# Hybrid pooling, stick-breaking and memory layer in fp32: memory attention's result parked in DRAM, its slots lent to the scores, and the last head pair's projections and pooling work reordered

## The chip, the cores and the metric

The kernel runs on one core of one Trainium2 chip. The metric is the device time of one execution in microseconds (us). The kernel before was timed three times: 543.44, 544.04 and 546.48 us, median 544.04 us. One more execution of it was taken with the hardware profiler.

## The reference

One decoder layer without its feed-forward half. `x` has 1024 tokens of 1024 channels, fp32. `h` is the RMS-normalised `x`, and one product `h @ W_in` gives all inputs of three mixers, whose outputs, each times SiLU of its gate, are concatenated, multiplied by `W_out` and added to `x`:

```
h = rmsnorm(x);  pool_v, pool_gate, sb_q, sb_k, sb_v, sb_gate, mem_q, mem_gate = split(h @ W_in)
A  pooling (256 channels, 4 groups of 64): windows of 2, 4, 8, 16 tokens:
     y = ((window_sum / count) - u) @ pool_w[group] * pool_scale
B  stick-breaking attention (8 heads of 64), strictly causal:
     z = q k^T / 8;  log_a = log_sigmoid(z) + sum over later keys of log_sigmoid(-z);  y = exp(log_a) @ v
C  memory attention (4 heads of 64): softmax over 256 memory tokens, RMS-normed q and k
out = x + concat(A*silu(gate), B*silu(gate), C*silu(gate)) @ W_out
```

## The kernel before, in words

**Numbers.** Every product is fp32 made of split parts: each operand is a high part plus a low part, and TensorE (PE) does high x high, high x low and low x high. A copy on ScalarE (ACT) makes the high part, a subtraction on VectorE (DVE) or GpSimd (POOL) the low one.

**Stages.** First come the norms, the transposes of `x` and the memory tokens' keys and values. Then memory attention (`mem_main`) runs among the first projections; its result stays in the slots `Y0` and `Y1` as `y_mem`. Then stick-breaking attention runs in four head pairs, p = 0 to 3, among the remaining projections. Last comes the output product, one level of Strassen-like recursion: seven products of 512x512 blocks (`oA`, `oS`, L1256 to L1258). Its sums of blocks are additions on DVE (L1232 `tt`; low parts L1226 `bs` and L1197 `hl`; sums of results L1267), and its operands `b_qa0`, `b_KA0`, `b_KB1` and so on are pieces of `W_out` that SP loads into slots that earlier stages have left (L1210).

**A projection unit** is 128 output columns of `h @ W_in`: two halves of 512 tokens with eight steps each, a step being three matmuls of 128x512 (L251, L254). `chain` loads the next unit's weights (SP, L152) in the first step of a unit, and splits them by quarters in later steps (ACT `wh` L277, POOL `wl` L278). Units are called `q`, `k`, `v`, `g` with the head pair (`v2`), `pv0`, `pv1` (the pooling values, two groups each), `pg0`, `pg1` (pooling gates) and `mg0`, `mg1` (memory gates).

**A score tile** (`be`, one head h, one block tb of 128 tokens, all keys up to it) goes this way. PE: `z` L754. ACT: sigmoid into a `be` buffer, L758. DVE: the running product along the keys, L767. For the head h = 1, DVE then transposes blocks of 32 (L769), SP stores the tile to DRAM (`zd`, L777) and reads it back transposed (`al`, L797 to L803), ACT makes the high part (L822) and POOL the low one (L823). For h = 0, PE transposes it (`ta` L593), ACT and DVE split it (L597, L598). PE: times `v` (`av`, L611). ACT and DVE: the result to `g_g`, where it meets the gate (L630, L633, L634). There are 64 score tiles, 16 for each pair. They take turns in four buffers with the tag `be`: a buffer comes free when its last reader (the store to DRAM, or PE's transposes) is done. Below, x counts score tiles from 0 in the order in which they get a buffer; x = 0 is the first of pair 0, x = 48 the first of pair 3.

**What sets the order.** `weave(main, fill, keep, lag)` puts attention's steps among the projection steps by planned costs: the last `keep` steps of the fill are left for the end, and the attention starts against a `lag`. `soon(us, fn)` defers vector work by planned microseconds. Inside the section `hand`, DVE, ACT, POOL and SP run in the order in which the code issues; behind `flush()` and `hand.close()` a scheduler places the vector work, and it may hoist the output product's work between that of the last pair. Each engine runs its list in order, so whatever waits at its head holds up what follows.

**The last pair** is woven with the units pv1, pg1, pv0, pg0, mg0. `pool_parts(r)` gives the pooling work of the unit pv r. `window_add` makes a window sum of twice the width from the last one: a copy of the first columns (L924, DVE) and an addition (L925). `mean` divides and subtracts (L936 to L939). ACT and POOL split the result (L944 `ph`, L947 `pl`), and `out_step` does the group's product (`py`, L964 to L966), whose result DVE multiplies by the gate (L969). The pooling works in slots that hold the output product's operands afterwards: `us` in `KA0`, `ps2` in `qa0`, `ph` in `qb0`. The unit mg writes a gate by `gate_unit` (L413, L416), and L418 multiplies `y_mem` by it.

Of the kernel before, what the change touches and what calls it, by code (L numbers as in the profile page):

```python
# [27 lines left out]
def layer_kernel(  # L28
# [305 lines left out]
    def k_unit(e0, name, tags):  # L334
        get = lazy(lambda: [slot2(t, f"{t}_{name}", dt=F32R)[:].rearrange("p (n s) -> p n s", n=2) for t in tags])

        def evac(th, c, pt):
# [12 lines left out]
            soon(0.9, low)  # L350
            soon(3.0, copy)

        return get, Unit(e0, name, evac)
# [530 lines left out]
    def pool_parts(r, gg):  # L884
# [27 lines left out]

        todo = []

        def window_add(n, c):
# [4 lines left out]
            prev, cur = (u if n == 0 else (s, s2)[(n - 1) % 2]), (s, s2)[n % 2]  # L920
            lo = HD if n == 2 * r + 1 else 0
            c0 = max(c.start, step)
            if c.start == 0:
                nc.vector.tensor_copy(cur[lo:P, 0:step], prev[lo:P, 0:step])  # L924
            (nc.gpsimd if [0, 0][r] else nc.vector).tensor_tensor(  # L925
                cur[lo:P, c0 : c.stop], prev[lo:P, c0 : c.stop], prev[lo:P, c0 - step : c.stop - step], op=ALU.add
            )
# [448 lines left out]
```

## Time and profile before

| | |
|---|---|
| median of three runs | 544.04 us (543.44 to 546.48) |
| the profiled execution, its own time | 546.15 us |
| span of the profiled execution, first to last instruction | 544.2 us |
| mean granted TensorE clock | 0.977 |
| PE busy | 506.1 us, 93% |
| DVE, ACT, POOL busy | 402.7, 296.5, 245.0 us |
| memory attention to the first scores of pair 0 | about 120 to 138 us |
| stick-breaking attention, pairs 0 to 3 | about 138 to 448 us, the heavy part of each at its end |
| output product | about 464 to 541 us |

The profiled execution took 2.11 us more than the median of the three runs, and 1.95 us of its time lie outside the span. Busy times of an engine are read against the span; a TensorE clock under 1.00 means that matmuls in that stretch ran slower than they can.

### The profile page before, as it was taken

The page shows a single profiled execution, that of the slowest core. Times are in us where ns is not written, and L with a number is a line of the kernel's source. Part 1 is how long each engine was busy: PE and PEld are TensorE (multiplying, and loading weights), DVE is VectorE, ACT ScalarE, POOL GpSimd, SP SyncE. Part 2 cuts the span into 40 slices and gives each one's busy share as a digit, 9 for nine tenths or more (in the row PEclk, how much of TensorE's full clock was granted, in tenths as well). Part 3 has the DMA queues.
Part 4 walks back from the last instruction along what each step waited for, and adds up shares of the span by engine and source line. Part 5 has one row for each costly group of instructions (what it writes and reads, how often), then busy time and mean ns, then how long its engine had stood idle before and what let it go on. Part 6 is the DMA issues. An engine that isn't in the chain of part 4 may idle for free.

```text
span 544.2 us, 7905 instructions
## 1 busy us (share of the span) xinstructions
PE 506.1 (93%) x2548; PEld 419.8 (77%) x2548; DVE 402.7 (74%) x627; ACT 296.5 (54%) x670; POOL 245.0 (45%) x239
## 2 busy tenths in 40 slices
PE   7889999999987999899999899996779989999997
PEld 6678888888865888688888688885657768888886
DVE  4777777786477955789855799558997588999663
ACT  6977756767354645564655465544643636563200
POOL 4570344445312363424745165454474753033980
PEclk9999999999998999989999899999899989999999
DMA  8910112435146633654664638643443432802123
GB/s 308 312 56 22 39 40 67 90 78 108 24 92 146 150 73 106 141 127 90 141 142 114 136 69 152 139 117 61 85 98 106 143 127 80 268 1 89 66 99 134
DMA packets 149504, 60.36 MB, mean 111 GB/s; under 512 B 104006, under 2 KB 139096, under 8 KB 149464
## 3 DMA queue, kind: packets, MB, share of 16 engines
q1 hardware_dynamic: 149464, 59.87, 43.0%
q8 instruction: 20, 0.33, 0.3%
q14 instruction: 20, 0.16, 0.1%
HBM read 39.92 MB, written 15.73 MB: 102 GB/s over the span
## 4 chain that ended last, share of the span: by engine, by line
PE 69%; DVE 9%; ACT 5%; issue 5%; DMA 4%; POOL 4%; SPq 2%; ACTq 0%; POOLq 0%; DVEq 0%
PE av L611 6%; PE u_q L254 5%; PE u_v L254 5%; PE u_g L254 5%; PE z L754 4%; DVE be L767 3%; PE u_k L254 3%; PE u_q L251 3%; PE u_g L251 3%; PE oS L1256 3%; PE oS L1258 3%; PE u_v L251 3%; PE oS L1257 3%; DMA zd<-be 2%; PE u_mg L254 2%
## 5 line engine op out<-in xcount | busy, mean ns | idle before, releaser
L767 DVE TENSOR_TENSOR_SCAN be<-be,later 128x128 f32<-128x128 f32 (+3 forms) x64 | 97.2, 1521 | 27.8 <-ACT be L758 27.2
L823 POOL TENSOR_TENSOR al<-al,ah 128x512 fp32r<-128x512 f32 (+1 forms) x40 | 56.9, 1425 | 71.2 <-ACT ah L822 56.9
L758 ACT ACTIVATE be<-z 128x128 f32<-128x128 f32 (+3 forms) x96 | 46.5, 490 | 64.7 <-PE z L754 27.2
L611 PE MATMUL av<-al,V_v 128*128 128x256 f32 (+1 forms) x160 | 33.3, 291 | 6.9 <-DVE al L598 5.3
L611 PEld LDWEIGHTS av<-ah,V_v 128*128 128x128 f32 x160 | 30.4, 195 | 11.2 <-issue 4.3
L598 DVE TENSOR_TENSOR al<-ta,ah 128x512 fp32r<-128x512 f32 (+1 forms) x40 | 25.2, 631 | 17.1 <-ACT ah L597 11.8
L754 PE MATMUL z<-KB_k,qb_q 128*128 128x512 f32 (+3 forms) x96 | 26.6, 362 | 9.1 <-ACT be L758 9.1
L611 PE MATMUL av<-ah,V_v 128*128 128x256 f32 (+1 forms) x160 | 31.0, 276 | 3.5 <-DVE g_g L634 3.5
L754 PE MATMUL z<-KA_k,qa_q 128*128 128x512 f32 (+3 forms) x96 | 27.3, 368 | 5.8 <-ACT be L758 5.8
L611 PEld LDWEIGHTS av<-al,V_v 128*128 128x128 f32 x160 | 25.1, 195 | 8.8 <-DVE al L598 6.6
L597 ACT ACTIVATE ah<-ta 128x512 fp32r<-128x512 f32 (+1 forms) x40 | 22.2, 556 | 15.8 <-PE ta L593 12.2
L630 ACT ACTIVATE avt<-av,ve_v 64x128 f32<-64x128 f32 x64 | 19.7, 356 | 19.7 <-PE av L611 11.2
L703 POOL TENSOR_SCALAR pe_m<-pe_m,nb_m 128x256 f32<-128x256 f32 x16 | 16.8, 1050 | 27.9 <-DVE nb_m L700 24.1
L754 PEld LDWEIGHTS z<-KB_k,qb_q 128*128 128x128 f32 x96 | 17.4, 193 | 15.4 <-ACT be L758 12.3
L251 PE MATMUL u_g<-hh,wh_g 128*128 128x512 f32 x64 | 27.6, 431 | 0.0
L822 ACT ACTIVATE ah<-al 128x512 fp32r<-128x512 f32 (+1 forms) x40 | 23.4, 584 | 6.6 <-DMA al<-zd 2.0
L251 PE MATMUL u_v<-hh,wh_v 128*128 128x512 f32 x64 | 26.8, 418 | 0.0
L251 PE MATMUL u_k<-hh,wh_k 128*128 128x512 f32 x64 | 26.4, 412 | 0.0
L754 PEld LDWEIGHTS z<-KA_k,qa_q 128*128 128x128 f32 x96 | 18.4, 200 | 10.2 <-ACT be L758 6.3
L278 POOL TENSOR_TENSOR wl_g<-wr_g,wh_g 128x256 fp32r<-128x256 f32 x16 | 13.8, 874 | 27.5 <-ACT wh_g L277 27.3
L1256 PE MATMUL oS<-bs,hh 128*128 128x512 f32 (+1 forms) x68 | 25.9, 381 | 0.0
L1258 PE MATMUL oS<-bs,hl 128*128 128x512 f32 (+1 forms) x68 | 25.8, 379 | 0.0
(322 smaller groups left out, 1601.7 us busy)
## 6 DMA issues: line engine op xcount, KB each, us to landing
al<-zd SPq DMA_DIRECT2D x24, 256.0 KB, 3.2
x<-in_x_dram SPq DMA_DIRECT2D x8, 512.0 KB, 6.3
wr_q<-in_w_in_dram SPq DMA_DIRECT2D x4, 512.0 KB, 4.0
wr_k<-in_w_in_dram SPq DMA_DIRECT2D x4, 512.0 KB, 4.0
wr_v<-in_w_in_dram SPq DMA_DIRECT2D x4, 512.0 KB, 3.8
KA_k<-KA_k SPq DMA_DIRECT2D x8, 256.0 KB, 3.3
KB_k<-KB_k SPq DMA_DIRECT2D x8, 256.0 KB, 3.6
wr_g<-in_w_in_dram SPq DMA_DIRECT2D x4, 512.0 KB, 3.9
```

The source lines that it names most:

```text
L251: nc.tensor.matmul(pt[:], wh[:, kc], hh[k][:, c], start=(k == 0), stop=False)
L254: nc.tensor.matmul(pt[:], w[:, kc], h[k][:, c], start=False, stop=(k == KD - 1 and n == 1))
L597: nc.scalar.activation(ah[:, :w], tp[:, :w], AF.Copy)
L598: low = lambda: nc.vector.tensor_tensor(al[:, :w], tp[:, :w], f(ah[:, :w]), op=ALU.subtract)
L611: nc.tensor.matmul(av[:, 256 - bw : 256], vs[n], part[:, o : o + bw], start=(first and part is ah and n == 0), stop=(last and part is al a ...
L754: nc.tensor.matmul(zp[:, 0:w], q[h][:, tcol], k[h][:, m, s0 : s0 + w], start=(m == 0), stop=(m == 1))
L758: nc.scalar.activation(t[:, s0 : s0 + w], zp[:, 0:w], AF.Sigmoid, scale=-(HD**-0.5))
L767: nc.vector.tensor_tensor_scan(t[:, rev], t[:, rev], mask, 1.0, op0=ALU.mult, op1=ALU.max)
L822: nc.scalar.activation(hi[:, 0:w], f(lo[:, 0:w]), AF.Copy)
L823: nc.gpsimd.tensor_tensor(lo[:, 0:w], f(lo[:, 0:w]), f(hi[:, 0:w]), op=ALU.subtract)
L1256: nc.tensor.matmul(bk[:, c], xh[:, tcol], wh[:, c], start=(n == 0), stop=False)
L1258: nc.tensor.matmul(bk[:, c], xl[:, tcol], wh[:, c], start=False, stop=(n == 3))
```

## The change

Seven edits:

1. `y_mem` is stored to DRAM after memory attention (`y_dr`, two stores of 512 KB), and read back as `y_back` into the same slots at step 56 of the last pair's units, ahead of the gates mg that multiply it.
2. In between `Y0` and `Y1` take score tiles: of the first 58, each sixth goes to `Y0` (x % 6 = 4) or `Y1` (x % 6 = 5). So six buffers take turns for x < 58, and four after that.
3. Planned delays grow: k's copies 3.0 to 5.0; v's store, load and split 3.6, 7.8, 13.0 to 4.4, 9.0, 15.0; the score's store 2.4 to 3.4.
4. Pairs 0 to 2 are woven with `keep` = 0 and `lag` = 0 in place of 4 and 1.0.
5. The last pair's units are pv1, pg1, pg0, pv0, mg0.
6. Pooling's vector steps are spread. Those of r = 1 go over unit steps 18 to 46 (before: one after each step from 22 to 35), with the products at 53 and 57. Those of r = 0 go over steps 64 to 77 (before: about 46 to 54), with both products behind step 79, the last.
7. The copy of a window sum's first columns goes from DVE to ACT, deferred by 2.0.

```
-            soon(3.0, copy)
+            soon(5.0, copy)
...
-            soon(3.6, store)
-            soon(7.8, load)
-            todo.append(soon(13.0, split))
+            soon(4.4, store)
+            soon(9.0, load)
+            todo.append(soon(15.0, split))
...
-                be[n, i] = slot("be", f"be_{name}")
+                x = n_be[0]
+                n_be[0] += 1
+                be[n, i] = slot("Y0" if x < 58 and x % 6 == 4 else "Y1" if x < 58 and x % 6 == 5 else "be", f"be_{name}")
...
-                soon(2.4 + 3.8e-3 * L, store)
+                soon(3.4 + 3.8e-3 * L, store)
...
-            if c.start == 0:
-                nc.vector.tensor_copy(cur[lo:P, 0:step], prev[lo:P, 0:step])
-            (nc.gpsimd if [0, 0][r] else nc.vector).tensor_tensor(
+            if c.start == 0 and n > 0:
+                heads[-1].run()
+            nc.vector.tensor_tensor(
                 cur[lo:P, c0 : c.stop], prev[lo:P, c0 : c.stop], prev[lo:P, c0 - step : c.stop - step], op=ALU.add
             )
+            if c.start == 0:
+                heads.append(soon(2.0, lambda: nc.scalar.activation(cur[lo:P, 0:step], prev[lo:P, 0:step], AF.Copy)))
...
+    for pr in range(2):
+        nc.sync.dma_start(y_dr[pr][:], y_mem[pr][:])
+    y_back = []
+
+    def y_load():
+        for pr in range(2):
+            y_back.append(slot(f"Y{pr}", f"y_back{pr}"))
+            nc.sync.dma_start(y_back[pr][:], y_dr[pr][:])
...
-    weave(attn[0], fill_0, 4, 1.0)
-    weave(attn[1], chain([u_q[2], u_k[2], u_g[2], u_v[2]], u_q[3]), 4, 1.0)
+    weave(attn[0], fill_0)
+    weave(attn[1], chain([u_q[2], u_k[2], u_g[2], u_v[2]], u_q[3]))
...
-    weave(attn[2], chain([u_q[3], u_k[3], u_g[3], u_v[3]], u_pv[1]), 4, 1.0)
-    fill = chain([u_pv[1], u_gp[1], u_pv[0], u_gp[0]]+[u_gm[0]], u_gm[1])
...
+    weave(attn[2], chain([u_q[3], u_k[3], u_g[3], u_v[3]], u_pv[1]))
+    units = chain([u_pv[1], u_gp[1], u_gp[0], u_pv[0], u_gm[0]], u_gm[1])
+
+    places = {}
+    for r, lo, hi, outs in ((1, 18, 46, (53, 57)), (0, 64.5, 77.5, (79.5, 79.7))):
...
+    places.setdefault(56, []).append((0.0, y_load))
```

Three places show how instructions move. The names: `be_p_h_tb_c` and `z_p_h_tb_c` are score tile and score piece of pair p, head h, token block tb, keys from 512 c on; the number at the end only tells tiles apart.

**ACT, the first heavy scores of pair 1** (x = 20 to 25), with the semaphores that each instruction waits for (`DMAHW` is a DMA queue's). Before:

```order
L758 ACTIVATE be_1_1_2_0_2446<-z_1_1_2_0_2443 128x384 [waits PE_49]
L277 ACTIVATE wh_g2_2401<-wr_g2_2336 128x256
L822 ACTIVATE ah_18_2456<-al_18_2371 128x512 [waits DMAHW3_49,Pool_49]
L758 ACTIVATE be_1_1_3_0_2462<-z_1_1_3_0_2459 128x512 [waits PE_49]
L340 ACTIVATE KA0_k2_2397<-u_k2_1_2406 64x512 [waits PE_49]
L340 ACTIVATE KB0_k2_2398<-u_k2_1_2406 64x512
L758 ACTIVATE be_1_0_2_0_2484<-z_1_0_2_0_2481 128x384 [waits DMAHW4_49,DMAHW5_49,DMAHW3_49,DMAHW6_49,DVE_49,PE_49]
L822 ACTIVATE ah_19_2488<-al_19_2414 128x384 [waits Pool_49]
L758 ACTIVATE be_1_0_3_0_2505<-z_1_0_3_0_2502 128x512 [waits PE_49]
L758 ACTIVATE be_1_1_4_1_2524<-z_1_1_4_1_2521 128x128 [waits PE_49]
```

The third, x = 22 (`be_1_0_2_0`), waits for a DMA: its buffer is that of x = 20 in the first row, and has to be stored to DRAM first. After:

```order
L760 ACTIVATE be_1_1_2_0_2458<-z_1_1_2_0_2455 128x384 [waits PE_49]
L824 ACTIVATE ah_18_2461<-al_18_2378 128x512 [waits DMAHW5_49,Pool_49]
L340 ACTIVATE KA0_k2_2389<-u_k2_1_2402 64x512 [waits PE_49]
L340 ACTIVATE KB0_k2_2390<-u_k2_1_2402 64x512
L760 ACTIVATE be_1_1_3_0_2474<-z_1_1_3_0_2471 128x512 [waits PE_49]
L760 ACTIVATE be_1_0_2_0_2499<-z_1_0_2_0_2496 128x384 [waits PE_49]
L824 ACTIVATE ah_19_2501<-al_19_2421 128x384 [waits DMAHW7_49,DMAHW6_49,Pool_49]
L760 ACTIVATE be_1_0_3_0_2507<-z_1_0_3_0_2504 128x512 [waits DMAHW1_49,DMAHW0_49,PE_49]
L760 ACTIVATE be_1_1_4_1_2530<-z_1_1_4_1_2527 128x128 [waits PE_49]
```

The same tile waits for PE alone: its buffer is that of x = 16, six score tiles earlier. The next, x = 23 (`be_1_0_3_0`), waits for the store of x = 17. In the kernel after, x = 58 (`be_3_0_4_1`), the first with four buffers again, still takes the buffer of x = 56, as before.

**DVE in the last pair, around the split `al_67`** (L598; L767, L769 are the scan and transpose before, L769, L771 after). Before:

```order
L767 SCALAR_TENSOR_TENSOR be_3_0_5_1_4112<-be_3_0_5_1_4112,later_147 128x768
L939 SCALAR_TENSOR_TENSOR us1_3734<-ps21_3899,cnt_160,us1_3734 64x512
L767 SCALAR_TENSOR_TENSOR be_3_1_6_1_4155<-be_3_1_6_1_4155,later_147 128x896
L769 STREAM_TRANSPOSE be_3_1_6_1_4155<-be_3_1_6_1_4155 128x896
L633 TENSOR_TENSOR av_43_4141<-av_43_4141,avt_3_0_1_4177 64x256
L634 TENSOR_TENSOR g_g3_3342<-g_g3_3342,av_43_4141 64x256
L598 TENSOR_TENSOR al_66_4214<-ta_66_4208,ah_66_4213 128x512
L767 SCALAR_TENSOR_TENSOR be_3_1_7_1_4190<-be_3_1_7_1_4190,later_147 128x1024
L769 STREAM_TRANSPOSE be_3_1_7_1_4190<-be_3_1_7_1_4190 128x1024
L633 TENSOR_TENSOR av_44_4198<-av_44_4198,avt_3_1_1_4233 64x256
L634 TENSOR_TENSOR g_g3_3342<-g_g3_3342,av_44_4198 64x256
L598 TENSOR_TENSOR al_67_4262<-ta_67_4256,ah_67_4261 128x512
```

A step of the mean of r = 1 over the second half of the tokens (L939, 64x512) stands between the scans there, and another in the row ahead of this piece. After, from the transpose ahead of `al_67` on:

```order
L771 STREAM_TRANSPOSE be_3_1_7_1_4186<-be_3_1_7_1_4186 128x1024
L416 TENSOR_TENSOR gp_3923<-u_pg0_0_4105,gp_3923 128x512
L941 TENSOR_TENSOR us1_3738<-ps21_3881,cnt_160 64x16
L942 TENSOR_TENSOR us1_3738<-us1_3738 64x16
L944 SCALAR_TENSOR_TENSOR us1_3738<-ps21_3881,cnt_160,us1_3738 64x496
L633 TENSOR_TENSOR av_44_4191<-av_44_4191,avt_3_1_1_4231 64x256
L634 TENSOR_TENSOR g_g3_3327<-g_g3_3327,av_44_4191 64x256
L598 TENSOR_TENSOR al_67_4261<-ta_67_4255,ah_67_4260 128x512
L769 SCALAR_TENSOR_TENSOR be_3_0_6_1_4239<-be_3_0_6_1_4239,later_147 128x896
L598 TENSOR_TENSOR al_68_4287<-ta_68_4282,ah_68_4286 128x384
L944 SCALAR_TENSOR_TENSOR ps21_3881<-us1_3738,cnt_160 64x512
L944 SCALAR_TENSOR_TENSOR us1_3738<-ps21_3881,cnt_160,us1_3738 64x512
```

These two steps (L944 now) stand behind `al_67` and `al_68`; the gate's addition L416 of pg0 and three steps of the mean's first half have come in ahead of `al_67`.

**POOL at the end of the last pair** (`al_76` to `al_79` are the last reads of attention, `wl_mg1` the weights of the last unit, `pl0` the low parts of the pooling r = 0, L947 before and L952 after). Before:

```order
L947 TENSOR_TENSOR pl0_4409<-us0_4239,ph0_4361 64x512
L278 TENSOR_TENSOR wl_mg0_4462<-wr_mg0_4384,wh_mg0_4461 128x256
L947 TENSOR_TENSOR pl0_4409<-ps20_4357,ph0_4361 64x512
L947 TENSOR_TENSOR pl0_4409<-us0_4239,ph0_4361 64x512
L278 TENSOR_TENSOR wl_mg0_4462<-wr_mg0_4384,wh_mg0_4461 128x256
L823 TENSOR_TENSOR al_76_4455<-al_76_4455,ah_76_4522 128x512
L278 TENSOR_TENSOR wl_mg0_4462<-wr_mg0_4384,wh_mg0_4461 128x256
L823 TENSOR_TENSOR al_77_4494<-al_77_4494,ah_77_4549 128x512
L823 TENSOR_TENSOR al_78_4517<-al_78_4517,ah_78_4570 128x512
L823 TENSOR_TENSOR al_79_4540<-al_79_4540,ah_79_4586 128x384
L278 TENSOR_TENSOR wl_mg1_4607<-wr_mg1_4556,wh_mg1_4606 128x256 x4
L1232 TENSOR_TENSOR b_V0_4721<-g_g0_1566 128x512
```

After:

```order
L825 TENSOR_TENSOR al_76_4444<-al_76_4444,ah_76_4505 128x512
L825 TENSOR_TENSOR al_77_4473<-al_77_4473,ah_77_4533 128x512
L902 MEMSET ps20_4537 128x128
L825 TENSOR_TENSOR al_78_4498<-al_78_4498,ah_78_4557 128x512
L909 TENSOR_TENSOR pw0_4536<-ps20_4537,pw0_4536 128x128
L825 TENSOR_TENSOR al_79_4522<-al_79_4522,ah_79_4578 128x384
L278 TENSOR_TENSOR wl_mg1_4588<-wr_mg1_4529,wh_mg1_4587 128x256 x4
L952 TENSOR_TENSOR pl0_4598<-ps20_4537,ph0_4541 64x512
L952 TENSOR_TENSOR pl0_4598<-us0_4428,ph0_4541 64x512
L952 TENSOR_TENSOR pl0_4598<-ps20_4537,ph0_4541 64x512
L952 TENSOR_TENSOR pl0_4598<-us0_4428,ph0_4541 64x512
L1250 TENSOR_TENSOR b_V0_4729<-g_g0_1566 128x512
```

All of `pl0` has moved from ahead of `al_76` to behind `wl_mg1`; on PE the products `py0_0` and `py0_1`, which read it, now stand directly behind the last step of the unit mg0, where before `py0_0` stood ahead of attention's last two products and `py0_1` in the middle of mg0's second half.

More of the change, by code (lines that the diff above doesn't have):

```diff
@@ L740, in sb_slots @@
         by_dma = [h == 1 for _, _, h in groups]
-        be, zd, wt, acc, stored = {}, {}, {}, {}, []
+        be, zd, wt, acc, stored, n_be = {}, {}, {}, {}, [], [0]
         def qk(n, i, c):
@@ L911, in weights @@
             box.extend([u, s, s2, slot("qb0", f"ph{r}", dt=F32R)])
-        todo = []
+        todo, heads = [], []
         def window_add(n, c):
@@ L931, in mean @@
             n = 2 * r + h
+            heads[-1].run()
             rows = slice(h * HD, (h + 1) * HD)
@@ L1136, in layer_kernel @@
     weave(mem_main(mq, y_mem), fill[9:], 4, 1.0)
+    y_dr = [dram.tile([P, 1024], F32, tag=f"yd{pr}", name=f"yd{pr}") for pr in range(2)]
+    for pr in range(2):
[5 more added lines that the diff above has]
+            nc.sync.dma_start(y_back[pr][:], y_dr[pr][:])
     hand = ExitStack()
@@ L1169, in layer_kernel @@
     hand.close()
-    mixed = [g() for g in gp] + [sb[p][3][0]() for p in range(4)] + y_mem
+    mixed = [g() for g in gp] + [sb[p][3][0]() for p in range(4)] + y_back
     half_e = [[2, 3, 4, 1], [0, 6, 5, 7]]
```

19 lines of the change are left out of this document (9 added, 10 removed).

## Prediction, made before the changed kernel was run

> **What bounds the kernel now.** I read the page first, then the waits of PE, then stretches of the span, then the single rows in which PE stands still.
>
> ```profile
> PE 506.1 (93%) x2548; PEld 419.8 (77%) x2548; DVE 402.7 (74%) x627; ACT 296.5 (54%) x670; POOL 245.0 (45%) x239
> ```
>
> PE is the bound: of the span of 544.2 us it is busy 506.1, so 38 us are idle, and nothing in the change removes a matmul. The gain can only come from idle time and from time at a lower clock. The waits of PE, and the wait of ACT that stands behind the first of them, say who is late (total, times, longest):
>
> ```profile
> PE z L754 <- ACT be L758: 14.9, 11, 4.0
> PE av L611 <- DVE al L598: 5.3, 5, 2.9
> PE u_mg L251 <- DVE gp L969: 2.3, 1, 2.3
> ACT be L758 <- DMA zd<-be: 19.1, 6, 6.0
> ```
>
> Scores wait for the sigmoid ahead of them, and that waits for a buffer whose score is still on its way to DRAM. The rows of ACT with that wait (start, duration, instruction, idle time before):
>
> ```profile
> 170.48 0.28 ACT L758 ACTIVATE be<-z 128x128 f32<-128x128 f32 x1 [5.99 <-DMA zd<-be]
> ...
> 230.05 0.49 ACT L758 ACTIVATE be<-z 128x384 f32<-128x384 f32 x1 [3.09 <-DMA zd<-be]
> ...
> 301.90 0.49 ACT L758 ACTIVATE be<-z 128x384 f32<-128x384 f32 x1 [3.06 <-DMA zd<-be]
> ...
> 381.88 0.28 ACT L758 ACTIVATE be<-z 128x128 f32<-128x128 f32 x1 [2.04 <-DMA zd<-be]
> ```
>
> The first three lie where the heavy scores of pairs 0, 1 and 2 set in, the last in the last pair. The stretches around them (length; busy time of PE, PEld, DVE, ACT, POOL; granted clock; DMA share):
>
> ```profile
> 150.00:160.00 10.00, 8.44 (x40) 6.60 (x39) 6.40 (x8) 4.04 (x9) 0.00 (x0) 1.00 0.52 119
> 160.00:165.00 5.00, 4.68 (x27) 3.66 (x26) 4.87 (x7) 3.97 (x10) 3.13 (x3) 1.00 0.39 95
> 165.00:172.00 7.00, 3.00 (x17) 2.44 (x15) 4.15 (x5) 1.50 (x4) 1.16 (x2) 0.94 0.82 159
> 172.00:176.00 4.00, 4.00 (x18) 3.38 (x17) 3.90 (x6) 2.52 (x8) 0.74 (x2) 0.68 0.26 49
> 225.00:230.00 5.00, 3.38 (x18) 2.56 (x16) 4.33 (x4) 1.18 (x2) 1.17 (x1) 1.00 0.79 171
> 230.00:236.00 6.00, 4.94 (x18) 4.03 (x19) 4.23 (x5) 2.78 (x7) 1.30 (x1) 0.72 0.65 154
> 300.00:304.00 4.00, 1.79 (x10) 1.10 (x8) 2.19 (x3) 1.12 (x3) 1.12 (x1) 1.00 0.85 150
> 304.00:310.00 6.00, 5.57 (x21) 4.70 (x22) 4.99 (x6) 3.04 (x9) 0.54 (x2) 0.72 0.48 114
> ```
>
> PE is idle 1.56, 0.32, 4.00, 0, 1.62, 1.06, 2.21 and 0.43 us in them: 11.2. Behind each stop the clock is lower; length times the missing share of the clock is 0.42 + 1.28, then 1.68, then 1.68: 1.7 us for each stop, 5.1 in all. Together the three places lose 16.3 us.
>
> The last pair is another matter. From the scan of x = 52 to the split al_67, without which PE can't go on, DVE is nearly full (41.19 of 43.25 us); the output product's stretch stands ahead of it in the answer, and gives the pace of PE at full clock: 49.00 us for 213 matmuls, 0.23 us each, so 0.7 us for a unit step or for a product `py`, of three matmuls each:
>
> ```profile
> 453.00:502.00 49.00, 49.00 (x213) 39.84 (x213) 48.80 (x72) 26.60 (x49) 10.08 (x8) 1.00 0.34 108
> 362.73:405.98 43.25, 31.32 (x154) 25.28 (x152) 41.19 (x52) 22.41 (x53) 21.95 (x16) 0.92 0.39 82
> ```
>
> **Boundaries of pairs 0 to 2** (six buffers; `keep` and `lag` 0). With six buffers x = 6, 22, 38 reuse a buffer from six scores back and not from two, so the DMA wait of these rows goes. What is late next is DVE, whose scans release the stores and transposes: in the same eight stretches it is idle 3.60 + 0.13 + 2.85 + 0.10, 0.67 + 1.77, and 1.81 + 1.01 us, 11.9 in all. Its work there is the same as before, so the stretch can shrink by what it idles and not much more, unless units spread into it let DVE lag. I take 12 us. The upper end is the whole 16.3. The lower end is 6.8: DVE's 11.9 less three half-clock stops of 1.7 that stay if PE then waits for DVE in pieces. The cover for the rest: ACT, at 1.50 of 7.00 us and 2.78 of 6.00 above, has room for the sigmoids.
>
> **The last pair up to al_67.** DVE sets the pace, so its own rows price the edits:
>
> ```profile
> 362.73 0.96 DVE L767 TENSOR_TENSOR_SCAN be<-be,later 128x384 f32<-128x384 f32 x1 [2.01 <-ACT be L758]
> ...
> 364.80 1.23 DVE L925 TENSOR_TENSOR us<-us 128x512 f32<-128x512 f32 x1
> ...
> 373.95 0.72 DVE L924 COPY us<-ps 128x4 f32<-128x4 f32 x1
> ...
> 379.50 0.17 DVE L924 COPY ps<-us 64x8 f32<-64x8 f32 x1
> ...
> 387.54 0.65 DVE L416 TENSOR_TENSOR gp<-u_pg,gp 128x512 f32<-128x512 f32 x1
> ...
> 390.68 1.46 DVE L939 SCALAR_TENSOR_TENSOR ps<-us,cnt 64x512 f32<-64x512 f32 x1
> ...
> 393.84 1.60 DVE L939 SCALAR_TENSOR_TENSOR us<-ps,cnt,us 64x512 f32<-64x512 f32 x1
> ...
> 405.29 0.69 DVE L598 TENSOR_TENSOR al<-ta,ah 128x512 fp32r<-128x512 f32 x1
> ...
> 410.69 0.75 DVE L969 SCALAR_TENSOR_TENSOR gp<-py,gcol,gp 128x512 f32<-128x512 f32 x1 [2.34 <-PE py L966]
> ```
>
> The copies of the heads leave DVE: 0.72 + 0.17, and about 0.1 for a third (an estimate). The addition of 1.23 us moves ahead of the scan, into the 2.01 us that DVE idles there. The two mean steps of 1.46 and 1.60 move behind al_67, where DVE now idles 2.34 us. In return a gate addition of 0.65 comes ahead of al_67. And DVE waited for the pooling weights:
>
> ```profile
> DVE ps L925 <- POOL pw L907: 2.8, 2, 1.5
> ```
>
> The longest, 1.5, is r = 0's at 419.56; the other 1.3 us is r = 1's and goes, as its weights now come earlier against its additions. The sum is 1.0 + 1.2 + 3.1 + 1.3 - 0.65 = 6 us. Bounds: 2.9 if the mean steps cost the same behind al_67 (the cover of 2.34 us gone), 8.0 if DVE's own 2.06 us of idle time go too. x = 58 still takes the buffer of x = 56, so the wait of 2.04 us at 381.88 stays, behind DVE's work.
>
> **The tail, from attention's end to the last unit.** What it loses now:
>
> ```profile
> 434.46 0.51 PE L611 MATMUL av<-al,V_v 128*128 128x256 f32 x2 [1.26 <-POOL al L823]
> ...
> 444.37 0.80 PE L251 MATMUL u_mg<-hh,wh_mg 128*128 128x512 f32 x1 [2.31 <-DVE gp L969]
> ```
> ```profile
> 444.00:450.00 6.00, 5.63 (x17) 4.35 (x18) 5.83 (x9) 2.08 (x6) 4.78 (x5) 0.72 0.00 0
> ```
>
> 1.26 + 2.31 + 1.7 for the clock = 5.3 us, which go: the low parts of r = 0 no longer stand ahead of al_76. But both products py0 now stand behind the last step of mg0, at E. ACT's sigmoid of that half waits for E, and three of the copies `ph` stand behind it; POOL's three low parts follow those:
>
> ```profile
> 427.33 0.63 ACT L944 ACTIVATE ph<-us 64x512 fp32r<-64x512 f32 x1
> ```
> ```profile
> 427.67 1.29 POOL L947 TENSOR_TENSOR pl<-us,ph 64x512 fp32r<-64x512 f32 x1
> ```
>
> The first is ready at about E + 0.6 + 0.6, the third low part at E + 1.4 + 3 x 1.29 = E + 5.3, and py0_1 (0.7 us, behind the last of them) ends at E + 6.0. Two products take 1.4 us anyway, so PE stands 4.6 us. To that comes half a half-clock stop, 0.85 as a middle, since two pieces of idle time of 2 to 3 us can bring one or none:
>
> ```profile
> 230.59 0.44 PE L754 MATMUL z<-KB_k,qb_q 128*128 128x128 f32 x2 [2.21 <-ACT be L758]
> ...
> 232.58 1.22 PE L754 MATMUL z<-KB_k,qb_q 128*128 128x512 f32 x2 [0.47 <-ACT be L758]
> ```
>
> A pause of 2.21 us and one of 0.47 already brought the clock of 0.72 in 230 to 236. The Trainium skill ("TensorE: Matmul & The Clock Gate", section "HAM oscillation — how this bites in real kernels") says that only PE-idle gaps over about 3.4 us cool the clock; this trace disagrees, with a longest pause of 2.21 us there. By that page the tail would pay no clock, 4.6 us and not 5.45. I go by the rows: 5.3 - 5.45 = -0.1, the tail is even. Bounds: +0.7 without a clock stop, -2.7 with two (4.6 + 3.4).
>
> **The output product.** Before, 16 of DVE's additions and low parts for it stand ahead of mg0's last addition, and its operands are loaded then; now none does, as `KA0`, `qa0`, `qb0` come free only after r = 0. The sixteen cost 0.6 to 0.7 us each:
>
> ```profile
> 437.39 0.78 DVE L1232 TENSOR_TENSOR b_KA<-b_KB,b_KA 128x512 f32<-128x512 f32 x1 [5.01 <-DMA b_KA<-in_w_out_dram]
> ...
> 442.97 0.68 DVE L1232 TENSOR_TENSOR b_KA<-b_KB,b_KA 128x512 f32<-128x512 f32 x1
> ```
>
> From mg1's start to the seventh product's sums the orders of before and after hold 61 and 62 instructions of DVE, because other additions have moved to the end; the products start with operands that need no addition, and the tightest low parts come about 1 us ahead of their need by these durations. I take a loss of 1 us. The bounds are 0 and 6 (the wait of 5.01 us once more, on the path).
>
> **Edits at nothing.** The result's store and reload are four transfers of 512 KB; the nearest row:
>
> ```profile
> x<-in_x_dram SPq DMA_DIRECT2D x8, 512.0 KB, 6.3
> ```
>
> The reload is issued at step 56, some 24 steps of 0.7 us = 17 us ahead of its first use, and lands in 6.3 to 12.6 us. If SP is late by more than 4 us, PE isn't held, but DVE's multiplication L418 is, and with it the output product. On SP the reload stands ahead of three reads of attention (al_77 to al_79), whose landing may slip by some 2 us. The longer delays of k, v and the scores only use slack behind the added buffers. Each: 0, within 1 us.
>
> **Sum.** 12 + 6 - 0.1 - 1 = 16.9 us against the profiled execution's own 546.15 us (span 544.2 and 1.95 outside): 529.2 us. That execution took 2.11 us more than the median; on the median this is 527 us. Fast and slow ends: 16.3 + 8 + 0.7 = 25 us, 519; 6.8 + 2.9 - 2.7 - 7 = 0, 544.
>
> **The rivals.**
>
> *The stops go whole.* If units spread into the heavy parts let DVE lag without holding PE, 16.3 + 8 + 0.7 = 25 us go: 519 us. For it: DVE is busy only 402.7 of 544.2 us. Against: 41.19 of 43.25 us.
>
> *DVE takes the place of the buffers.* If PE waits for scans at each boundary, 6.8 + 2.9 - 2.7 - 1 = 6 us are left: 538 us. For it: 5.3 us of waits for L598 already.
>
> *It doesn't do what it says.* If the extra buffers are held by the result's store, or the stores' longer delay of 1.0 us eats their gain, the waits stay: 544 us. Against: the first tile that needs `Y0` is the fifth, and the nearest 512 KB transfer of the same kind took 6.3 us.
>
> *Slower: DVE can't take the output product's work back.* Place: 453 to 502, where DVE is busy 48.80 of 49.00 us. If the sixteen (16 x 0.69 = 11 us) don't hide behind PE, operands wait for their loads (5.0), and the tail pays 4.6 + 3.4, then 24 us are lost; with boundaries at DVE's bound (6.8 + 2.9) and the old tail's 5.3 gained, the time is 544 + 24 - 15 = 553 us. It decides from the point where the product's loss exceeds the 15 us gained, i.e. if PE stands over 7 us in the product beyond the tail's 8. Against: PE is busy 49.00 of 49 there, and the counts 61 and 62.
>
> **How the numbers follow.** My forecast, 527 us, has 0.60 (its own range 521 to 534). The stops go whole: 0.15. DVE in the buffers' place: 0.12. No effect: 0.05. Slower: 0.08. The range from 517 to 539 us holds the forecast, most of the first rival and of the second, and leaves out about 2 in 10. About 0.5% is what a measurement of this kernel can tell from no change. Faster by over 0.5%: 0.60 + 0.15 + 0.12 = 0.87; the same: 0.05; slower: 0.08.
>
> **What would show it.** Right: no row "ACT be <- DMA zd<-be" over 1 us in pairs 0 to 2, no clock of 0.68 or 0.72 at their boundaries, the DVE stretch to al_67 near 37 us, a stop of 4 to 5 us ahead of py0_1 on PE, and PE full in the output product. Wrong: stops of PE for L598 or L767 at the boundaries, py0 waiting for the mean's steps on DVE, or idle PE between the seven products.

## The result, and the profile after

The changed kernel takes 528.16 us (median of four runs, 527.97 to 528.56); the kernel before, beside it, 545.26 us. The ratio is 0.969, with a 95% interval from 0.965 to 0.973: about 17 us less. The profiled execution has a span of 526.2 us; before it was 544.2.

The first part of the page of the kernel after:

```profile
PE 499.3 (95%) x2548; PEld 416.4 (79%) x2548; DVE 403.4 (77%) x621; ACT 300.6 (57%) x676; POOL 248.2 (47%) x239
```

PE has as many matmuls as before (x2548); its idle time fell from 38 to 27 us. The waits of PE after (total, times, longest):

```profile
PE av L611 <- DVE al L598: 6.1, 4, 3.5
PE py L970 <- POOL pl L952: 3.3, 2, 2.0
...
PE z L754 <- ACT be L760: 2.7, 3, 1.7
...
PE py L969 <- ACT ph L949: 1.3, 1, 1.3
```

The first wait of before, 14.9 us behind the sigmoids, is down to 2.7; the splits of DVE (L598) lead now, and the products `py` wait for their low parts, as they had not before. The stretches in which the three boundaries lie now:

```profile
150.00:160.00 10.00, 10.00 (x48) 8.23 (x48) 7.59 (x10) 5.37 (x11) 0.67 (x2) 1.00 0.54 118
160.00:170.00 10.00, 10.00 (x58) 8.64 (x57) 9.80 (x11) 7.69 (x20) 5.04 (x5) 1.00 0.67 151
225.00:236.00 11.00, 11.00 (x64) 9.54 (x64) 10.70 (x14) 7.80 (x20) 5.46 (x5) 1.00 0.66 125
300.00:310.00 10.00, 10.00 (x55) 8.48 (x54) 9.84 (x11) 6.13 (x14) 5.02 (x4) 1.00 0.46 93
```

PE is full and the clock 1.00 in all of them.

For the accounts both spans are cut at the same places of the program: first score, first step of pg1, split al_67, first and last matmul of the output product. Before:

```profile
137.64:355.60 217.96, 205.90 (x1057) 171.83 (x1055) 156.76 (x191) 117.66 (x274) 92.73 (x85) 0.98 0.53 115
355.60:405.29 49.69, 38.45 (x191) 31.33 (x189) 42.80 (x57) 25.41 (x60) 25.36 (x19) 0.93 0.39 88
405.29:463.56 58.27, 53.05 (x242) 42.78 (x242) 43.58 (x65) 28.14 (x57) 31.07 (x27) 0.94 0.39 115
463.56:540.78 77.22, 77.22 (x348) 63.63 (x347) 62.27 (x88) 25.12 (x45) 35.67 (x24) 1.00 0.32 111
```

After:

```profile
138.42:338.79 200.37, 199.22 (x1056) 168.62 (x1055) 154.02 (x191) 118.43 (x273) 92.01 (x84) 1.00 0.59 129
338.79:385.21 46.42, 38.16 (x194) 31.06 (x192) 43.04 (x51) 26.06 (x64) 21.62 (x18) 0.96 0.54 122
385.21:445.50 60.29, 53.53 (x239) 43.23 (x240) 40.19 (x54) 29.26 (x61) 35.78 (x30) 0.89 0.40 121
445.50:522.50 77.00, 77.00 (x349) 63.58 (x347) 68.56 (x98) 26.52 (x46) 38.61 (x24) 1.00 0.29 99
```

Pairs 0 to 2 gain 17.6 us, the heavy part of the last pair 3.3, the tail loses 2.0, the output product is the same within 0.2. The first score is 0.8 us later and the end 0.3 longer: 18.0 us of span. The cuts are at the same places of the program, but not quite at the same work of PE: 194 matmuls for 191 now stand in the heavy part, 239 for 242 in the tail.

### The profile page after: what moved, and what is told of

It reads as the page before. It is cut to its first block, busy times and chain, and to the rows that moved or that the text cites. A ratio compares the mean times of both kernels' runs of the same rounds, so it can differ in the third digit from the quotient of the medians.

```text
span 526.2 us, 7899 instructions
## 1 busy us (share of the span) xinstructions
PE 499.3 (95%) x2548; PEld 416.4 (79%) x2548; DVE 403.4 (77%) x621; ACT 300.6 (57%) x676; POOL 248.2 (47%) x239
## 4 chain that ended last, share of the span: by engine, by line
PE 70%; DVE 11%; ACT 6%; issue 4%; POOL 4%; DMA 3%; SPq 1%; DVEq 0%; POOLq 0%; ACTq 0%
PE av L611 6%; PE u_q L254 6%; PE u_k L254 5%; PE u_g L254 5%; DVE be L769 5%; PE u_v L254 4%; PE z L754 4%; PE u_q L251 3%; PE oS L1274 3%; PE oS L1276 3%; PE oS L1275 3%; PE u_k L251 3%; PE u_g L251 2%; PE u_pv L254 2%; PE oA L1274 2%
## 5 line engine op out<-in xcount | busy, mean ns | idle before, releaser
L769 DVE TENSOR_TENSOR_SCAN be<-be,later 128x128 f32<-128x128 f32 (+3 forms) x64 | 97.8, 1533 | 15.0 <-ACT be L760 14.8
L825 POOL TENSOR_TENSOR al<-al,ah 128x512 fp32r<-128x512 f32 (+1 forms) x40 | 61.4, 1537 | 44.0 <-ACT ah L824 40.2
L598 DVE TENSOR_TENSOR al<-ta,ah 128x512 fp32r<-128x512 f32 (+1 forms) x40 | 25.2, 630 | 17.1 <-ACT ah L597 15.4
L630 ACT ACTIVATE avt<-av,ve_v 64x128 f32<-64x128 f32 x64 | 19.8, 357 | 17.6 <-PE av L611 9.5
L754 PE MATMUL z<-KA_k,qa_q 128*128 128x512 f32 (+3 forms) x96 | 25.7, 352 | 2.7 <-ACT be L760 2.7
L251 PE MATMUL u_g<-hh,wh_g 128*128 128x512 f32 x64 | 26.5, 415 | 0.0
L1274 PE MATMUL oS<-bs,hh 128*128 128x512 f32 (+1 forms) x68 | 25.9, 380 | 0.0
L771 DVE STREAM_TRANSPOSE be<-be 128x128 f32<-128x128 f32 (+7 forms) x32 | 24.9, 779 | 1.1
L1275 PE MATMUL oS<-bs,hh 128*128 128x512 f32 (+1 forms) x68 | 25.6, 377 | 0.0
L692 ACT ACTIVATE pe_m<-z_m,nb_m,qsc 128x256 f32<-128x256 f32 x32 | 17.8, 561 | 13.5 <-DVE nb_m L688 11.0
```

The lines of the kernel that those rows point to most:

```text
L251: nc.tensor.matmul(pt[:], wh[:, kc], hh[k][:, c], start=(k == 0), stop=False)
L598: low = lambda: nc.vector.tensor_tensor(al[:, :w], tp[:, :w], f(ah[:, :w]), op=ALU.subtract)
L754: nc.tensor.matmul(zp[:, 0:w], q[h][:, tcol], k[h][:, m, s0 : s0 + w], start=(m == 0), stop=(m == 1))
L769: nc.vector.tensor_tensor_scan(t[:, rev], t[:, rev], mask, 1.0, op0=ALU.mult, op1=ALU.max)
L771: nc.vector.transpose(t[:, 0:L], t[:, 0:L])
L825: nc.gpsimd.tensor_tensor(lo[:, 0:w], f(lo[:, 0:w]), f(hi[:, 0:w]), op=ALU.subtract)
```

## The experiments

Ratios are to the kernel before, measured beside it on the same chip; the changed kernel's is 0.969 (0.965 to 0.973).

**Which edit carries the boundaries.** Four kernels. `buffers_only` is the kernel before with the two lent slots and the result's way to DRAM and back:

```
-                be[n, i] = slot("be", f"be_{name}")
+                be[n, i] = slot("Y0" if x < 58 and x % 6 == 4 else "Y1" if x < 58 and x % 6 == 5 else "be", f"be_{name}")
```

> The kernel before with the six score buffers alone (the result's store, its reload at step 56, and the two slots lent to the scores; delays, weave, last pair and pooling as before). Theory 1, the buffers: the three boundary stops (11.2 us of idle PE and 5.1 us of clock) came from buffer reuse alone, so 14 to 16 us of the 17 go: about 530 us. Theory 2, the spreading: without units spread into the heavy parts, PE waits for the scans there instead, and at most 5 us go: about 540 us, with waits of PE for L598 or the scans at the boundaries.

530.57 us, ratio 0.973 (0.968 to 0.977): 14.8 us, as theory 1 said. But theory 2 has a part in it. The boundaries and what follows them in this kernel:

```profile
150.00:176.00 26.00, 25.54 (x130) 20.85 (x129) 23.71 (x26) 17.46 (x38) 10.16 (x7) 1.00 0.67 148
225.00:236.00 11.00, 11.00 (x64) 9.45 (x62) 10.71 (x14) 7.24 (x19) 2.32 (x4) 1.00 0.75 158
300.00:310.00 10.00, 9.87 (x52) 8.25 (x51) 9.80 (x12) 7.69 (x20) 5.72 (x5) 1.00 0.50 85
176.00:192.00 16.00, 14.13 (x67) 11.65 (x66) 13.93 (x16) 7.33 (x18) 6.85 (x5) 0.89 0.54 114
```

The boundaries are nearly as full as in the changed kernel. DVE falls behind, and PE pays for it some 10 to 20 us later, here with 1.87 us of idle time and 16 x 0.11 = 1.8 us of clock in 176 to 192. Its first part, first score to pg1, takes 206.2 us: 11.8 less than before, where the changed kernel gains 17.6.

`four_buffers` is the changed kernel without the lent slots, the store and the reload:

```
-                be[n, i] = slot("Y0" if x < 58 and x % 6 == 4 else "Y1" if x < 58 and x % 6 == 5 else "be", f"be_{name}")
+                be[n, i] = slot("be", f"be_{name}")
```

> The changed kernel with four score buffers (no store or reload of memory attention's result, all scores in be). Theory 1: the boundary stops come back, 14 to 17 us: about 543 us. Theory 2: spread units cover them, at most 5 us come back: 530 to 533 us.

537.43 us, ratio 0.984 (0.981 to 0.987): 9 us come back, between the two theories. Its ACT still waits for the stores as before (18.6 us; 19.1 before), but PE loses less by it:

```profile
PE z L754 <- ACT be L760: 9.6, 13, 2.4
```
```profile
ACT be L760 <- DMA zd<-be: 18.6, 6, 4.7
```

`old_weave` is the changed kernel with the old weave of pairs 0 to 2:

```
-    weave(attn[0], fill_0)
+    weave(attn[0], fill_0, 4, 1.0)
```

(and the two like it)

> The changed kernel with keep 4 and lag 1.0 in pairs 0 to 2. Theory 1: the weave matters little once the buffers are there: 528 to 530 us. Theory 2: the spreading carries the boundary's gain: 536 us or more.

533.46 us, ratio 0.977 (0.974 to 0.980): the weave is worth about 5 us on top of the buffers, which theory 1 had at 0 to 2 and theory 2 at 8 or more. PE's waits for L598 come back at 184.70, 253.54 and 321.10 us (1.86, 0.67 and 0.63 us), some 10 to 20 us behind the boundaries, as in `buffers_only`:

```profile
184.70 0.51 PE L611 MATMUL av<-al,V_v 128*128 128x256 f32 x2 [1.86 <-DVE al L598]
```

`keep4_only` splits the edit, with keep 4 and lag 0:

```
-    weave(attn[0], fill_0)
+    weave(attn[0], fill_0, 4, 0.0)
```

> The changed kernel with keep 4 and lag 0 in pairs 0 to 2 (the run old_weave had keep 4 and lag 1.0: 533.5 us). Theory: the four unit steps left for each pair's end are what DVE lacked as cover, so this is 533 us, with PE's waits for al behind DVE at 184, 253 and 321 us. Rival: the lag of 1.0 did it: 528 to 529 us.

531.66 us, ratio 0.975 (0.972 to 0.978), its interval over that of `old_weave`. Its first wait of PE for L598:

```profile
184.54 0.50 PE L611 MATMUL av<-al,V_v 128*128 128x256 f32 x2 [1.85 <-DVE al L598]
```

The same wait at 251.8 and 319.7 us is 0.65 and 0.62. PE idles as long in the first part as in `old_weave` (3.9 and 3.8 us). What differs is the clock: the wait at 184 us was followed by a clock of 0.86 over the 12 us from 180 in `old_weave`, 1.7 us lost, and of 1.00 here. So the four units kept for the end carry the weave's worth, and the lag adds nothing that these two runs show. In the kernel after, one of 1.00 is left in all three pairs:

```profile
172.79 0.45 PE L611 MATMUL av<-al,V_v 128*128 128x256 f32 x2 [1.00 <-DVE al L598]
```

What follows: in the whole kernel the buffers alone are worth 14.8 us, all other edits without them 8 to 9, together 17; but the last pair's edits are in these sums. In the first part alone, first score to pg1, it is 11.8 us for the buffers, 7.1 for the rest without them (`four_buffers`; 5.0 in `parked_only` below, which lost 3.4 us more of clock), and 17.6 together: within the clock's chance, buffers and weave add up. The weave alone, in the kernel before, was not run.

**The parking itself.** `parked_only` keeps the store and the reload, but no score uses the slots:

```
-                be[n, i] = slot("Y0" if x < 58 and x % 6 == 4 else "Y1" if x < 58 and x % 6 == 5 else "be", f"be_{name}")
+                be[n, i] = slot("be", f"be_{name}")
```

> The changed kernel with the result stored to DRAM and read back, but no score in its two slots (four score buffers). Against the run four_buffers (537.4 us), which lacks store and reload, it prices the four transfers alone. The prediction priced them at nothing: 537 to 538 us. Rival: the reload of 1 MB holds attention's last reads on the DMA queues: 539 us or more.

538.86 us, ratio 0.989 (0.986 to 0.993), against 0.984 (0.981 to 0.987) of `four_buffers`. The medians differ by 1.4 us, the ratios by 0.5% (2.6 us), the intervals overlap, and the time is close to the rival's 539. But it is not the reload: from al_67 to the output product the two profiles take 59.8 and 59.3 us. The first part takes 212.9 and 210.9, with the same idle time of PE (8.3 and 8.4 us). What differs there is the clock: `parked_only` has two half-clock stops of 1.7 us, behind gaps of 1.87 us at 159.30 and 2.30 at 172.74, and `four_buffers` has none, though it has a gap of 2.44 at 171.18. The stretch of the second stop in `four_buffers`, then in `parked_only`:

```profile
165.00:180.00 15.00, 12.11 (x65) 9.81 (x65) 12.96 (x14) 8.59 (x20) 6.22 (x5) 1.00 0.74 163
```
```profile
165.00:180.00 15.00, 12.55 (x61) 10.40 (x61) 12.96 (x16) 8.29 (x21) 5.53 (x5) 0.89 0.81 176
```

So no idle time is seen that the four transfers cost by themselves. Whether they shifted the gaps so that the clock fell isn't shown.

**The delays.** `old_delays` sets all five back:

```
-            soon(5.0, copy)
+            soon(3.0, copy)
...
-                soon(3.4 + 3.8e-3 * L, store)
+                soon(2.4 + 3.8e-3 * L, store)
```

> The changed kernel with all five planned delays as before. The prediction priced them at nothing: 528 us, within 1. Rival: SP issues the scores' stores before DVE's transposes are done and holds the other loads, so that waits for DMAs come back at the pair boundaries: 531 us or more.

528.00 us, ratio 0.969 (0.967 to 0.970): nothing, as predicted.

**The last pair.** `old_last_pair` has the order of units and the pooling's places as before, the rest as changed:

```
-    units = chain([u_pv[1], u_gp[1], u_gp[0], u_pv[0], u_gm[0]], u_gm[1])
+    fill = chain([u_pv[1], u_gp[1], u_pv[0], u_gp[0]]+[u_gm[0]], u_gm[1])
```

> The changed kernel with the last pair's units, pooling places and products as before (pv1, pg1, pv0, pg0, mg0; head copies stay on ACT). By the traces of before and after the heavy part of the last pair gained 3.3 us and the tail lost 2.0 us, so the two cancel nearly: about 529 us (528 to 531). Rival, the heavy part is where the reorder pays and the tail's stop is the scheduler's: 532 us or more. Other rival, the tail's stop weighs more: 526 us or less.

528.46 us, ratio 0.970 (0.965 to 0.974): no difference that this interval resolves. The four times are 526.62, 526.70, 530.22 and 530.25 us, and the profile is of the first. In it the heavy part takes 48.65 us at a mean clock of 0.89 and the tail 56.55 at 0.97; the changed kernel's are 46.42 at 0.96 and 60.29 at 0.89. What edits 5 and 6 gain by al_67 they lose behind it.

`r1_close` puts the steps of the first pooling group back together:

```
-    for r, lo, hi, outs in ((1, 18, 46, (53, 57)), (0, 64.5, 77.5, (79.5, 79.7))):
+    for r, lo, hi, outs in ((1, 22, 35, (53, 57)), (0, 64.5, 77.5, (79.5, 79.7))):
```

> The changed kernel with the first pooling group's vector steps over unit steps 22 to 35, as before, and not 18 to 46. By the prediction the two mean steps then stand ahead of al_67 again: 3.1 us later, 531 us. By the trace of after these steps take 0.73 us each when POOL rests, and 1.5 us only where POOL's low parts run beside them, so they cost 1.5 us there: 529 to 530 us. If the low parts' place matters more than the count of DVE steps: 528 us or less.

531.14 us, ratio 0.974 (0.972 to 0.975): 3.0 us slower, the prediction's price, but as the net of two larger sizes. The two mean steps stand ahead of al_67 again and take 1.44 and 1.67 us, the 3.1 predicted; additions take 2.2 us more there, and the heavy part is 51.7 us, 5.3 more. The tail is 56.6, 3.7 less, most of it clock (0.94 over the tail, 0.89 in the changed kernel: 3.4 and 6.6 us lost).

`heads_on_dve` puts the copies of the first columns on DVE again:

```
-                heads.append(soon(2.0, lambda: nc.scalar.activation(cur[lo:P, 0:step], prev[lo:P, 0:step], AF.Copy)))
+                heads.append(soon(0.0, lambda: nc.vector.tensor_copy(cur[lo:P, 0:step], prev[lo:P, 0:step])))
```

> The changed kernel with the copies of the first columns on DVE again, right behind each first addition. By the prediction's rows they cost DVE about 1.0 us in the full stretch: 529 us. Rival, they are hidden: 528 us, within 0.5. Other rival, ACT's copies hold DVE up: 527 us.

529.37 us, ratio 0.971 (0.969 to 0.972): 1.2 us by the medians, and 0.9 us in the heavy part of the profile (47.3 for 46.4); the intervals overlap.

**The tail.** `early_weights` loads the last group's weights earlier and sets its steps closer:

```
+            at_ = 58 if r == 0 and n == 0 else int(lo + n * (hi - lo) / len(todo))
...
-    for r, lo, hi, outs in ((1, 18, 46, (53, 57)), (0, 64.5, 77.5, (79.5, 79.7))):
+    for r, lo, hi, outs in ((1, 18, 46, (53, 57)), (0, 64.0, 72.0, (79.5, 79.7))):
```

> The changed kernel with the last pooling group's weights loaded at step 58 in place of 64, and its vector steps over steps 64 to 72 in place of 64 to 77; both products stay behind step 79. Theory of the tail: the stop ahead of py0 (1.34 + 1.97 + 1.37 us of idle PE, and about 3 us of half clock in and behind it) is set by this chain on DVE, ACT and POOL, which lost 3.14 us to the weights; then 4 to 7 us go: 521 to 524 us. Rival, the stop is set by POOL's low parts behind the last weights' split alone: under 2 us go, 526 to 528 us.

526.75 us, ratio 0.965 (0.964 to 0.967): 1.4 us, the rival's size. DVE and ACT are done with the group 5.7 and 4.6 us sooner, but POOL's low parts now stand between the quarters of the last unit's weights (L278), and the last of them ends at 429.55 us where it ended at 431.16. The rows of POOL:

```profile
424.43 1.27 POOL L952 TENSOR_TENSOR pl<-us,ph 64x512 fp32r<-64x512 f32 x1
425.78 1.21 POOL L278 TENSOR_TENSOR wl_mg<-wr_mg,wh_mg 128x256 fp32r<-128x256 f32 x1
426.95 1.26 POOL L952 TENSOR_TENSOR pl<-ps,ph 64x512 fp32r<-64x512 f32 x1
428.29 1.26 POOL L952 TENSOR_TENSOR pl<-us,ph 64x512 fp32r<-64x512 f32 x1
```

`low_on_dve` makes these low parts on DVE:

```
-                nc.gpsimd.tensor_tensor(pl[rows, c], dst[rows, c], f(ph[rows, c]), op=ALU.subtract)
+                (nc.gpsimd if r else nc.vector).tensor_tensor(pl[rows, c], dst[rows, c], f(ph[rows, c]), op=ALU.subtract)
...
-            todo.append(soon(3.3, high))
-            todo.append(soon(4.4, low))
+            todo.append(soon(3.3 if r else 1.0, high))
+            todo.append(soon(4.4 if r else 2.4, low))
```

> The kernel of the run early_weights with the low parts of the last pooling group on DVE in place of POOL, and its high and low parts 1.0 and 2.4 behind the mean (3.3 and 4.4 before). Theory: the stop ahead of py0 (1.21 + 2.88 us idle in early_weights, and about 3 us of half clock) is POOL's four low parts between the last weights' split; on DVE they take 0.7 us each and are done before the last step of mg0, so 4 to 6 us go: 521 to 523 us. Rival: DVE, which then is full from here to the middle of the output product, gives the time back there: 525 to 527 us.

526.66 us, ratio 0.966 (0.963 to 0.969): nothing, and by neither theory's way. The low parts are ready at 427 us, but the scheduler has put the output product's first split, which waits for its operand's load, ahead of the sigmoid of mg0's second half, behind which DVE frees the product's PSUM bank. The wait on ACT, and PE's behind it:

```profile
427.92 0.63 ACT L1244 ACTIVATE bs<-b_qa 128x512 fp32r<-128x512 f32 x1 [3.58 <-DMA b_qa<-in_w_out_dram]
428.45 0.58 ACT L413 ACTIVATE g_mg<-u_mg 128x512 f32<-128x512 f32 x1
```
```profile
430.05 0.80 PE L969 MATMUL py<-ph,pw 128*128 128x512 f32 x1 [4.71 <-DVE g_mg L416]
```

`py_in_mg1` leaves `early_weights` as it is and moves the two products into the last unit:

```
+    m1 = u_gm[1].steps
+    fill += m1[:4] + po[0][-2:-1] + m1[4:7] + po[0][-1:]
+    weave(attn[3], fill, 13, 3.0)
...
-    run(u_gm[1].steps[:8])
+    run(u_gm[1].steps[7:8])
```

> The kernel of the run early_weights with the two products py0 behind the fourth and the seventh step of the last unit mg1 in place of ahead of it, so that POOL's low parts have 3 to 5 us of matmuls as cover. Theory: the tail's stop (1.21 + 2.88 us idle, about 3 us of half clock) goes and the output product starts on time: 520 to 523 us. Rival: the output product's first operands, loaded into the slots that the products read, come later than the shorter tail needs them, and PE waits there instead: 525 to 527 us.

523.81 us (523.54 to 524.08), ratio 0.960 (0.957 to 0.963): 4.3 us faster than the changed kernel, 2.9 faster than `early_weights`, and the fastest of all. Both theories hold in part. Its stretches from al_67 to the product, and the product:

```profile
383.73:437.16 53.43, 51.89 (x242) 42.51 (x242) 38.40 (x48) 26.54 (x56) 37.12 (x30) 0.94 0.42 123
437.16:518.01 80.85, 77.92 (x348) 63.45 (x347) 76.20 (x108) 29.09 (x51) 36.97 (x25) 1.00 0.32 113
```

The tail is 6.9 us shorter than in the changed kernel, and the product 3.9 longer. PE now waits for the split operands in it:

```profile
444.13 0.49 PE L1277 MATMUL oA<-bs,hh 128*128 128x512 f32 x1 [1.22 <-ACT bs L1246]
445.16 0.50 PE L1278 MATMUL oA<-bs,hh 128*128 128x512 f32 x1 [0.54 <-DVE bs L1247]
463.10 0.50 PE L1278 MATMUL oA<-bs,hh 128*128 128x512 f32 x1 [1.18 <-DVE bs L1247]
```

## Why the prediction was right, and which steps of it were not

The forecast of 527 us for 528.16, 17 us for 17, is right in the whole because wrong sizes cancel, and that is luck: in the profiles the boundaries gave 5.6 us more than forecast, the heavy part 2.7 less, the tail 1.9 less, the output product 1.2 more, and the first score and the end, which the sum left out, took 1.1.

*Boundaries: predicted 12 us, measured 17.6.* That buffer reuse makes the stops, and that six buffers take them away, is shown by `buffers_only` and its full stretches. The step that failed is "the stretch can shrink by what it idles and not much more, unless units spread into it let DVE lag". DVE did lag, in both kernels: it doesn't bind where it is full, but where PE next needs its last result. In `buffers_only` that bill comes later in the pair (1.87 us of idle time and 1.8 of clock in pair 0), and 11.8 us remain, near the 12 by luck. The weave edit, which the prediction had as part of the same 12, lets DVE catch up under matmuls: about 5 us more by `old_weave`, 3.5 by `keep4_only`, which was spared a half-clock stop. The first rival, "the stops go whole", was right in this part: 17.6 us for its 16.3. The 1.3 us above that aren't accounted for.

*Heavy part of the last pair: predicted 6 us, measured 3.3.* The work that goes was named rightly: from the scan of x = 52 to al_67, by start-to-start times on DVE, mean steps fall by 2.75 us (3.1 predicted), additions by 0.73 (1.2), copies by 0.74 (1.0), idle time by 1.25 (1.3), and the gate's addition costs 0.65. That is 4.8. But the ten scans there take 18.42 us for 16.96, 1.5 more, with nothing changed in them. A scan of 128x512 after, the rows of POOL beside it, and a scan of the same shape before:

```profile
348.02 2.10 DVE L769 TENSOR_TENSOR_SCAN be<-be,later 128x512 f32<-128x512 f32 x1
```
```profile
347.75 1.29 POOL L825 TENSOR_TENSOR al<-al,ah 128x512 fp32r<-128x512 f32 x1
349.01 1.37 POOL L909 TENSOR_TENSOR pw<-ps,pw 128x128 fp32r<-128x128 f32 x1
```
```profile
365.95 1.21 DVE L767 TENSOR_TENSOR_SCAN be<-be,later 128x512 f32<-128x512 f32 x1
```

POOL rested from 365.5 to 368.9 there. In the fourteen profiles of this case, 88 scans of this shape stand singly in the timelines: the 38 without POOL beside them took 1.18 to 1.23 us, the 50 with it 1.18 to 2.34, and 33 of these over 1.3. So a slow scan has POOL beside it each time, though POOL doesn't slow each scan; that POOL is the cause is not tried by itself. The Trainium skill ("GPSIMD Engine Reference", section "1. Specifications") says that GpSimd's SBUF interfaces are shared with VectorE, with contention where VectorE's instruction runs in a two-port mode or has two SBUF inputs. The scan reads two, `be` and `later`, and these rows agree, 2.10 for 1.21 us.

*Tail: predicted even, measured 2.0 us lost.* The idle time ahead of py0_1 came out as forecast, 4.6 predicted, 1.34 + 1.97 + 1.37 = 4.68 measured:

```profile
425.73 0.49 PE L969 MATMUL py<-ph,pw 128*128 128x512 f32 x1 [1.34 <-ACT ph L949]
428.19 0.79 PE L970 MATMUL py<-pl,pw 128*128 128x512 f32 x1 [1.97 <-POOL pl L952]
428.79 0.63 PE L971 MATMUL py<-ph,pw 128*128 128x512 f32 x1
429.21 0.63 PE L969 MATMUL py<-ph,pw 128*128 128x512 f32 x1
431.21 0.80 PE L970 MATMUL py<-pl,pw 128*128 128x512 f32 x1 [1.37 <-POOL pl L952]
```

That it matches is luck too. Four low parts and not three follow E (424.4 us), at 1.26 to 1.71 us each; the last ends at E + 6.8 for the E + 5.3 worked out, and the six matmuls of py0, at the lower clock, fill 3.2 us of it for 1.4.

The term that was mis-sized is the clock, "half a half-clock stop, 0.85 as a middle". The stretches around it show three:

```profile
424.00:432.00 8.00, 3.33 (x8) 1.72 (x7) 5.28 (x8) 2.48 (x4) 6.87 (x5) 0.66 0.13 41
432.00:440.00 8.00, 8.00 (x27) 6.36 (x26) 6.11 (x7) 5.33 (x9) 5.45 (x4) 0.70 0.84 253
```

8 x 0.34 + 8 x 0.30 = 5.1 us, three times 1.7. Part of it falls on idle PE. The last unit takes 13.3 us from its first matmul (432.23) to the output product for the 11.2 of before, and with py0's six matmuls, 3.2 for 1.4, PE loses 3.9 us to the clock where 0.85 was priced. That is 3 us more than forecast for the new stop, and the tail came out 1.9 worse: about 1 us isn't accounted for. In it are a wait of 0.91 us for DVE (at 415.99 before) that is gone, and one for POOL's `al` that was to go (1.26 before) and is there again, 1.34 us at 396.38. The Trainium skill's rule that there be no PE-idle gaps over about 3.4 us ("TensorE: Matmul & The Clock Gate", section "HAM oscillation — how this bites in real kernels"), taken as the price, would have made this term nothing. The trace disagrees: the longest gap here is 1.97 us.

*Output product: predicted a loss of 1 us, measured none.* PE is full from 445.5 to 522.5. The slower rival needed PE to stand over 7 us in the product, and it doesn't stand there at all; `py_in_mg1` shows that its mechanism is near: with 6.9 us less of tail the operands are late, and PE idles 2.9 us in the product. (The slow end of the sum takes 7 us at this place, while the bound worked out for it is 6; with 6 that end is 543 us.)

*Edits at nothing.* The delays were worth nothing. The result's way to DRAM shows no idle time of its own (`parked_only`). The weave was priced inside the boundaries' 12 us.

## What to carry to other kernels

A wait on a buffer is priced by following its release chain; but an engine that looks full in the same stretch need not be the next bound there. Ask where its results are next needed, and whether the schedule gives it cover until then: here the buffers alone gave 11.8 us of the first part, the rest alone 5 to 7, and both 17.6. And work pushed to a stage's end pays at the seam: moving the two products under the last unit's matmuls gave back 2.9 us (`early_weights` to `py_in_mg1`).

## What the runs showed of the hardware

What a stop of PE cost in clock came in steps of 1.7 us in these profiles, and the length of its gaps doesn't tell how many. The 4.1 to 5.3 us of idle time ahead of py0 came in one piece of 4.71 us (`low_on_dve`), in two of 1.21 and 2.88 (`early_weights`), and in three of about 1.34, 2.0 and 1.4 to 1.9 (the changed kernel and seven others). The two stretches 424 to 432 and 432 to 440 us, of `low_on_dve`:

```profile
424.00:432.00 8.00, 3.29 (x11) 2.32 (x10) 6.29 (x11) 1.96 (x5) 3.09 (x4) 0.87 0.56 195
432.00:440.00 8.00, 8.00 (x33) 6.43 (x32) 6.68 (x8) 5.36 (x9) 5.29 (x4) 0.92 0.84 263
```

and of `early_weights`:

```profile
424.00:432.00 8.00, 3.91 (x12) 2.51 (x11) 3.93 (x7) 1.60 (x3) 6.84 (x7) 0.80 0.32 112
432.00:440.00 8.00, 8.00 (x29) 6.32 (x28) 8.00 (x9) 5.86 (x11) 4.82 (x3) 0.77 0.91 315
```

The missing clock is 8 x (0.13 + 0.08) = 1.7 us in one piece and 8 x (0.20 + 0.23) = 3.4 in two. In three pieces it is 5.1 in the changed kernel; a kernel with nearly the same three pieces, `four_buffers`, loses 16 x 0.21 = 3.4 (`r1_close`, `old_delays`, `old_weave`, `keep4_only` and `parked_only` show the same 0.79 over 16 us, and `heads_on_dve` 0.68 as the changed kernel):

```profile
433.00:449.00 16.00, 11.24 (x38) 8.10 (x37) 11.40 (x15) 8.23 (x15) 12.34 (x9) 0.79 0.47 152
```

Inside such a stop the granted clock reads 0.50 (429 to 436 us in the changed kernel), hence the name half-clock stop. Single gaps show the same. Those of 2.30 and 2.44 us above cost 1.7 us and nothing, and the wait for L598 at 184 us took 1.87 us in `buffers_only`, 1.86 in `old_weave` and 1.85 in `keep4_only`, and cost 1.7 us of clock in the first two and nothing in the third. This looks like a count over fixed stretches of time that a stop may straddle or not; no run tries that. The Trainium skill has it so ("TensorE: Matmul & The Clock Gate", section "What's actually happening": the clock is set by a window of 3413 ns that runs freely); the steps of 1.7 us, half of such a window, agree. One piece cost one step here, two pieces two, three pieces two or three, in one profile of each kernel; that the number of pieces decides isn't tried by itself.
